# The RWKV recurrence of a decoder trunk as 64 by 64 tiles of the array, both heads of a pair together

## The chip, the cores and the metric

The kernel runs on one core of one Trainium2 chip. The metric is the device time of one execution in microseconds: 2238.92 us, the median of 3 runs (2235.21 to 2239.05). The profile shows one further execution of its own.

A core has TensorE (PE, with its weight loads listed apart as PEld), VectorE (DVE), ScalarE (ACT), GpSimd (POOL), and SyncE, whose queue (SP) issues the DMAs here. PE multiplies from SBUF into PSUM, which holds eight banks of 128 partitions by 512 float32 values.

## The reference, cut to what matters

The kernel computes a trunk of two layers on 512 positions of 1024 features. Each layer adds half a SwiGLU feed-forward, a mixer, and half a feed-forward again. The mixer of layer 0 is RWKV-7 with 12 heads of 64, beside an attention of 4 heads to a memory of 256 positions; that of layer 1 is a dilated attention and the same kind of memory attention. The part that the change rewrites is the recurrence of layer 0:

```python
def step(state, inp):
    r_t, w_t, k_t, v_t, kk_t, a_t = inp
    sa = jnp.einsum('bhvk,bhk->bhv', state, -kk_t)
    state = (state * w_t[:, :, None, :]
             + sa[..., None] * (kk_t * a_t)[:, :, None, :]
             + v_t[..., None] * k_t[:, :, None, :])
    return state, jnp.einsum('bhvk,bhk->bhv', state, r_t)
```

Its state is 64 by 64 for each head. The outputs are then normalised by head, get a bonus term, and are gated.

## The kernel before

Everything is feature-major: a tile is 128 features (two heads of 64) by 512 positions. The feed-forward layers (`ffn`) and the projections (`dense`, line 399) split each float32 operand into two halves of 12 bits and take three products of whole 128 by 128 blocks with 512 columns; one step of `dense` issues three such matmuls and yields. They read as `fps` (feed-forward) and `mm` (mixer) in the profile. The small products of the recurrence are plain float32 matmuls, and each of them leaves two records of PE.

The mixer of layer 0 (`mixer_a`, line 584) handles the 12 heads as 6 pairs, one pair to a tile of 128 features. It is written as strands, Python generators that emit instructions in steps: `projections` (key, receptance and value of pair j), `prepare` (decay, normalised keys, everything by position, `rwkv_prepare`, line 728), two strands `scan(0)` and `scan(1)` that run `rwkv_solve` (line 801) on the first and the second head of each pair, `finish` (`rwkv_finish`, line 865), two strands of memory attention, and a first pass of the output projection. `weave` (line 294) emits each time the first strand whose next step can start by the clock of `Meter` (line 216), which adds up an estimated cost of each instruction (`cost`, line 225). All strands share the PSUM banks `mm` (2), `sc` (4) and `py` (2). The pairs are coupled: `prepare` of pair j waits until the output of pair j-2 is there (line 683), the projections of pair j wait until pair j-2 is prepared, and `finish` takes the pairs one by one.

The recurrence is cut into 8 chunks of 64 positions; a block is two chunks, 128 positions. For one head, `rwkv_solve` does this:

- Products within the chunks (`AR` with `beta` and `kappa`): 64 by 64 tiles, whose results are masked by DVE onto the diagonal squares of 128 by 128 matrices (`products`, the profile's `prod`) that are zero elsewhere and were cleared once at the start.
- The inverse of a triangular matrix by doubling (`LEVELS`, 2 to 32): at each of five levels DVE turns 32 by 32 squares of `TT`, PE multiplies by `MA` for each of the four blocks (128 by 128, the profile's `sc<-tx,prod`), DVE masks, PE multiplies again (`sc<-TT,tx`), and DVE adds.
- `SA` (the turned `AR` of this head, and what the chunk reads of its own values), and `wu`, the solution for both.

`rwkv_finish` turns `beta` and `kappa` to positions on partitions, in a copy for each chunk of a block with zeros in the other chunk's rows (`betatok`, `kappatok`), and for each head in turn: the readout matrices (`pt`), the transitions `G`, and what each chunk adds to the state, gathered in the `py` bank. A loop over the chunks then carries the state of both heads: PE multiplies `G` by `H`, ACT scales into the next `H` (one copy a head), PE reads out. Group norm, bonus and gate follow.

Of the kernel before, what the change touches and what calls it, by code (L numbers as in the profile page):

```python
# [17 lines left out]
P = 128  # L18
# [5 lines left out]
HD = 64  # L24
# [12 lines left out]
# ---------------------------------------------------------------- constants of shapes alone  # L37
# [12 lines left out]
def constants():  # L50
    f = np.float32
    i = np.arange(P)
    same = (i[:, None] // HD == i[None, :] // HD).astype(f)
    s, t = i[:, None], i[None, :]
    chunk = s // C == t // C
    strict, incl = (chunk & (s < t)).astype(f), (chunk & (s <= t)).astype(f)
    lvl = []
    for b in LEVELS:
        lvl.append(((s // (2 * b) == t // (2 * b)) & (s // b % 2 == 1) & (t // b % 2 == 0)).astype(f))
    first = ((s // 2 == t // 2) & (s % 2 == 0) & (t % 2 == 1)).astype(f)  # L60
    ident = np.eye(P, dtype=f)
    stack = np.concatenate([np.eye(HD, dtype=f)] * 2, 0)
    cols = [ident, same, 1.0 - same, np.ones((P, P), f), strict, incl, first, *lvl, stack]
# [17 lines left out]
CONST_W = [P, P, P, P, 2 * P, P, *([P] * len(LEVELS)), HD]  # L81
# [10 lines left out]
def swapped(n):  # L92
    """Feature order with the two heads of each 128-row tile exchanged."""
# [50 lines left out]
# ---------------------------------------------------------------- kernel  # L144
# [17 lines left out]
def wide(t):  # L162
    return t.unsqueeze(1).broadcast_to([P, 4, P])
# [6 lines left out]
class Operand:  # L170
    """Both halves of x * gain for each 128 features, and the sum of squares of x, as the tiles of x come."""
# [31 lines left out]
    def rstd(self, ps):  # L203
        """1 / sqrt(mean over features + eps) on every partition."""
# [11 lines left out]
class Meter:  # L216
    """Estimates when each engine gets through what has been emitted, to choose the order of emission."""

    def __init__(self):
# [3 lines left out]
        self.banks = set()  # L223

    def cost(self, engine, op, out, ins, extra):
        """extra: operands that are one value per partition, and sums over the free size."""
# [4 lines left out]
        if engine == "tensor":  # L231
# [3 lines left out]
            return max(n * passes * 0.000417 * (0.6 if out.shape[0] < P else 1), 0.055) + 0.003  # L235
# [24 lines left out]
    def follow(self, slots, n, tile):  # L260
        """The tile takes the place of the one n tiles before it in slots."""
# [22 lines left out]
class Core:  # L284
    """The engines, with a meter on each."""
# [44 lines left out]
class Net:  # L330
# [30 lines left out]
    def warm(self):  # L361
        """The table of the first activations, ahead of their data."""
# [17 lines left out]
    # -- weights: one chunk is [128, nb, 128]; both halves of each value  # L380
# [34 lines left out]
    def split_into(self, hi, lo, src, gain=None):  # L415
        """hi + lo = src * gain exactly, each of 12 bits."""
# [8 lines left out]
    def add_state(self, old, j, ps, nexts, dst, scale=None, permute=False, x=None):  # L425
        """Tile j of x, to the operands that follow and to DRAM. scale: half of what the columns of ps lack."""
# [14 lines left out]
    # -- x + 1/2 SwiGLU(x)  # L441
# [46 lines left out]
    # -- keys and values of the memory  # L488
# [13 lines left out]
    def memory_kv(self, layer, tmp, bank, operand, out):  # L502
        """out: keys [128, 2, 256] by feature and values [128, 2, 256] by position."""
# [19 lines left out]
    def head_norm(self, out, t, gain, tmp, bank, n):  # L523
        """RMS norm over the 64 rows of each head."""
# [58 lines left out]
    # -- layer 0: RWKV-7 and memory attention  # L583
    def mixer_a(self, xin, u, kv, mid, nexts, dst, after):
        nc, tc = self.nc, self.tc
        w = self.ap["wa_in"]
        with ExitStack() as ctx:
# [10 lines left out]
            self.tok = {}  # L598
            for n in ("beta", "kappa"):
                self.tok[n] = pool.tile([P, 4, 2, P], F32, name=f"{n}tok")  # L600
                nc.gpsimd.memset(self.tok[n], 0.0)

            # zero outside the chunks' squares
            self.products = [[pool.tile([P, 4, 2, P], F32, name=self.nm("prod")) for _ in range(2)] for _ in range(2)]
            for two in self.products:
                for t in two:
                    nc.gpsimd.memset(t, 0.0)

# [14 lines left out]
            self.lora = {}  # L623
            self.krv = [None] * NPAIR
# [4 lines left out]
            def shifted(ps, m, out):  # L629
                """Projection m over the rms, mixed with the position before."""  # L630
# [7 lines left out]
            def projections():  # L638
# [89 lines left out]
    def rwkv_prepare(self, j):  # L728
        """Decay, keys and the rest by position, for heads 2j and 2j + 1."""
# [6 lines left out]
        # E[., c, t] is the decay over chunk c before position t, Ei the inverse of that after it  # L736
        zw = self.bank("sc")
        pe.matmul(zw, lora[:HD, 0], self.lo[:HD], start=True, stop=True)
# [3 lines left out]
        yield WAIT  # L742
        za = self.bank("sc")
        pe.matmul(za, lora[HD:, 0], self.lo[HD:], start=True, stop=True)
# [56 lines left out]
    def rwkv_solve(self, j, e):  # L801
        """What the chunks of head 2j + e read of the state at their start and of their own values."""
# [4 lines left out]
        mine, vals = own(e), own(1 - e)  # L807
        # products within the chunks, on the diagonal of MA[:, block] = A_b', A_k' and MB[:, block] = B_b', B_k'
        MA, MB = self.products[e]
        for b0 in (0, 2):  # L810
            ps = self.bank("sc", (P, 2, 2, 2, C))
            for b in range(2):
                for q, t in enumerate((beta, kappa)):
                    for c in range(2):
                        at = (b0 + b) * P + c * C
                        pe.matmul(ps[own(c), b, q], t[mine, at:at + C], AR[mine, b0 + b, :, own(c)], start=True,
                                  stop=True, skip_group_check=True)
            yield FREE
            for i, m in enumerate((MA, MB)):
                for c in range(2):  # L820
                    mask = self.mprod[own(c), i * P + c * C:i * P + (c + 1) * C]
                    vec.tensor_tensor(m[own(c), b0:b0 + 2, :, own(c)], ps[own(c), :, :, i],
                                      mask.unsqueeze(1).unsqueeze(1).broadcast_to([C, 2, 2, C]), op=ALU.mult)
            yield FREE
        yield WAIT
        ps = self.bank("sc", (P, 4, P))
        for b in range(4):
            pe.transpose(ps[:, b, :HD], AR[mine, b, 0], self.ident[mine, mine])
        SA = self.big("SA", 2, (P, 4, P))
        act.activation(SA[:, :, mine], ps[:, :, :HD], AF.Copy)  # L830
        # inverse of I - A_b by doubling the blocks of its diagonal
        TT = self.big("TT", 2, (P, 4, P))
        gp.tensor_tensor(TT, MA[:, :, 0], wide(self.first), op=ALU.mult)
        gp.tensor_tensor(TT, TT, wide(self.ident), op=ALU.add)
        yield WAIT
        for lv in LEVELS:
            # blocks of at most 32 lie on the diagonal: turning each 32 by 32 square turns the whole
            tn = self.big("tx", 3, (P, 4, P))
            vec.transpose(tn.rearrange("p b u -> p (b u)"), TT.rearrange("p b u -> p (b u)"))
            yield WAIT  # L840
            ps = self.bank("sc", (P, 4, P))
            for b in range(4):
                pe.matmul(ps[:, b], MA[:, b, 0], tn[:, b], start=True, stop=True, skip_group_check=True)
            X = self.big("tx", 3, (P, 4, P))
            vec.tensor_tensor(X, ps, wide(getattr(self, f"lvl{lv}")), op=ALU.mult)
            yield WAIT
            ps = self.bank("sc", (P, 4, P))
            for b in range(4):
                pe.matmul(ps[:, b], X[:, b], TT[:, b], start=True, stop=True, skip_group_check=True)
            vec.tensor_tensor(TT, TT, ps, op=ALU.add)  # L850
            yield WAIT
        ps = self.bank("sc", (P, 4, P))
        for b in range(4):
# [367 lines left out]
```

## Time and profile before

| | us |
|---|---|
| runs: median (lowest, highest) | 2238.92 (2235.21, 2239.05) |
| the profiled execution: its span | 2236.6 |
| layer-0 mixer, first projection to the start of its last outputs | 385 to 880 |
| `bv` written, the last step of `prepare`, first and last pair | 441.5, 775.5 |
| layer-1 mixer, about | 1640 to 1880 |

The span lies 2.3 us under the median of the runs. The page counts PE, its weight loads and the three other engines as busy by the union of their instructions. A record's length is a latency; records overlap, also on one tile of the array, so what one costs is the distance to the start of the next. In the groups, the numbers after the count are the group's busy time and the mean length of one record in ns. The form `64*64` names the rows and columns of the array that a matmul uses; `sc<-TT,tx` names what it writes and reads. A helper records every operation, so all instructions carry its line (L276). The rows that carry the argument stand in the prediction.

### The profile page before, as it was taken

To read this page: it belongs to the slowest core of one execution; us is meant where nothing else is said; L and a number is where in the kernel's file an instruction comes from. 1 tells how busy PE (TensorE), PEld (TensorE's weight loads), DVE (VectorE), ACT (ScalarE), POOL (GpSimd) and SP (SyncE) were. 2 spreads that over 40 slices of the span, in tenths; PEclk is the share of its full clock that TensorE was granted. 3 is DMA by queue.
4 is the path that set the end of the run, shared out by engine and by line. 5 is a ranking of instruction groups with operands and counts; after the bars stand their busy time and mean duration, and the time that the engine had idled before them with its cause. 6 is when DMAs were issued, how large, how long until landed. Compare 5 with 4: busy or idle time off the path is not lost.

```text
span 2236.6 us, 29471 instructions
## 1 busy us (share of the span) xinstructions
PE 2206.0 (99%) x11174; PEld 1779.8 (80%) x11174; DVE 1066.1 (48%) x1556; ACT 843.8 (38%) x1492; POOL 603.3 (27%) x520
## 2 busy tenths in 40 slices
PE   8999999999999999999999999999999999999999
PEld 6888888688777877778888888888877677888887
DVE  5333334576877874633343443333355675333332
ACT  6333333323323444433343343333334544333321
POOL 2222223632333113322222222222232224222221
PEclk9999999989999999999999999999999999999999
DMA  5333344200100005436334443333451125333342
GB/s 195 98 96 95 104 136 139 76 24 22 32 28 13 12 22 180 153 95 182 95 109 132 136 136 98 96 96 113 134 143 52 41 90 191 100 98 96 94 137 80
DMA packets 130621, 221.97 MB, mean 99 GB/s; under 512 B 14232, under 2 KB 31824, under 8 KB 130480
## 3 DMA queue, kind: packets, MB, share of 16 engines
q1 hardware_dynamic: 130480, 220.09, 32.6%
q8 instruction: 88, 1.44, 0.3%
q14 instruction: 53, 0.43, 0.1%
HBM read 203.15 MB, written 21.61 MB: 100 GB/s over the span
## 4 chain that ended last, share of the span: by engine, by line
PE 94%; DVE 3%; ACT 1%; POOL 1%; issue 1%; DMA 1%; SPq 0%; POOLq 0%; ACTq 0%; DVEq 0%
PE fps L276 65%; PE sc L276 14%; PE mm L276 12%; PE py L276 4%; DVE tmp L276 1%; DVE tx L276 0%; DVE prod L276 0%; DVE krv L276 0%; POOL wlo L276 0%; ACT uh L276 0%; POOL sq L276 0%; DMA raw<-w 0%; DMA x<-xT 0%; DVE x L276 0%; DMA tmp<-xd 0%
## 5 line engine op out<-in xcount | busy, mean ns | idle before, releaser
L276 POOL TENSOR_TENSOR wlo<-raw,whi 128x512 fp32r<-128x512 f32 (+3 forms) x404 | 496.6, 1231 | 1460.3 <-ACT whi L276 1427.8
L276 ACT ACTIVATE whi<-raw 128x512 fp32r<-128x512 f32 (+3 forms) x684 | 416.3, 610 | 943.9 <-PE fps L276 787.3
L276 PE MATMUL fps<-uh,whi 128*128 128x512 f32 x1408 | 551.5, 392 | 8.3 <-ACT whi L276 8.3
L276 PE MATMUL fps<-uh,wlo 128*128 128x512 f32 x1408 | 550.6, 391 | 2.3 <-POOL wlo L276 2.1
L276 PE MATMUL fps<-ul,whi 128*128 128x512 f32 x1408 | 548.9, 390 | 0.0
L276 DVE TENSOR_TENSOR wlo<-raw,whi 128x512 fp32r<-128x512 f32 x280 | 199.8, 714 | 344.5 <-ACT whi L276 333.3
L276 PEld LDWEIGHTS fps<-uh,whi 128*128 128x128 f32 x1408 | 264.9, 188 | 68.5 <-ACT whi L276 11.7
L276 PEld LDWEIGHTS fps<-uh,wlo 128*128 128x128 f32 x1408 | 264.9, 188 | 61.6 <-POOL wlo L276 5.3
L276 PEld LDWEIGHTS fps<-ul,whi 128*128 128x128 f32 x1408 | 264.8, 188 | 55.4 <-issue 0.7
L276 PE MATMUL fps<-hh,whi 128*128 128x512 f32 x704 | 273.9, 389 | 0.0
L276 PE MATMUL fps<-hl,whi 128*128 128x512 f32 x704 | 273.9, 389 | 0.0
L276 PE MATMUL fps<-hh,wlo 128*128 128x512 f32 x704 | 273.9, 389 | 0.0
L276 DVE TENSOR_TENSOR gs<-fps,rstd 128x512 f32<-128x512 f32 x88 | 60.5, 690 | 324.5 <-PE fps L276 324.5
L276 PEld LDWEIGHTS fps<-hh,wlo 128*128 128x128 f32 x704 | 132.1, 188 | 27.7
L276 PEld LDWEIGHTS fps<-hh,whi 128*128 128x128 f32 x704 | 132.1, 188 | 27.5
L276 PEld LDWEIGHTS fps<-hl,whi 128*128 128x128 f32 x704 | 132.1, 188 | 27.1
L276 PE MATMUL mm<-uh,whi 128*128 128x512 f32 x280 | 121.3, 434 | 1.5 <-ACT uh L276 1.1
L276 PE MATMUL mm<-ul,whi 128*128 128x512 f32 x280 | 117.9, 421 | 0.0
L276 DVE TENSOR_TENSOR hm<-fps,gs 128x512 f32<-128x512 f32 x88 | 60.6, 691 | 120.1 <-PE fps L276 115.8
L276 PE MATMUL mm<-uh,wlo 128*128 128x512 f32 x280 | 115.0, 411 | 0.0
L276 DVE RECIPROCAL tmp<-tmp 128x128 f32<-128x128 f32 x112 | 99.4, 920 | 16.6 <-ACT tmp L276 16.5
L276 DVE TENSOR_TENSOR hl<-hm,hh 128x512 fp32r<-128x512 f32 x88 | 77.5, 883 | 50.7 <-ACT hh L276 50.6
(256 smaller groups left out, 2612.2 us busy)
## 6 DMA issues: line engine op xcount, KB each, us to landing
raw<-w SPq DMA_DIRECT2D x512, 256.0 KB, 2.7
raw<-wa_in SPq DMA_DIRECT2D x44, 256.0 KB, 2.8
xd<-x SPq DMA_DIRECT2D x40, 256.0 KB, 2.5
tmp<-xd SPq DMA_DIRECT2D x32, 256.0 KB, 3.4
xin<-xd SPq DMA_DIRECT2D x32, 256.0 KB, 4.3
raw<-w_kv SPq DMA_DIRECT2D x24, 256.0 KB, 3.0
raw<-w SPq DMA_DIRECT2D x32, 128.0 KB, 2.4
raw<-wmem SPq DMA_DIRECT2D x16, 256.0 KB, 2.7
```

Source lines behind the costliest of these rows:

```text
L276: r = f(*args, **kw)
```

## The change

The recurrence goes to 64 by 64 tiles of the array throughout, and both heads of a pair are done together, side by side in the columns of a tile.

- `rwkv_solve(j)` takes a pair. Positions of a chunk of either half of a block lie on partitions 0 to 63 or 64 to 127, the heads beside each other along the columns. The products of `beta`, then of `kappa`, fill one bank for each head and are masked by one DVE operation a head into `mb` and `mk`; the cleared 128 by 128 matrices are gone. `TT`, its transposes and its masks are `[128, 8, 64]` for both heads. Each level is 16 products of 64 by 64 in place of 4 of 128 by 128 a head, on the two diagonal tiles of the array, into one bank.
- The transposes of `beta` and `kappa` move from `rwkv_finish` into `rwkv_solve`, without the zero rows. `SA` is one tile for both heads with a flag `shared` around its use; `AR` is turned whole.
- `rwkv_finish` computes `pt` and `G` for both heads in two banks `kg`, one for each half of the blocks, and gathers readouts and state terms in two banks `py`, again one for each half. In the state loop ACT makes one copy `H` of 128 partitions a step for both heads.
- The strands `scan(0)` and `scan(1)` take the even and the odd pairs in place of the first and the second heads.
- In `rwkv_prepare` the products `zw` and `za` are issued next to each other.
- `Meter.cost` has no factor 0.6 for narrow outputs, a least cost of 0.105 in place of 0.055, a division by the number of tiles that a block of code declares with `packed`, and 0.1 for each change between packed and other matmuls. It also plans the mixer of layer 1.
- The masks in the block of constants are 64 columns wide in place of 128 (1088 columns in all, from 1600). Comments are removed.

```diff
@@ Meter.cost
-            return max(n * passes * 0.000417 * (0.6 if out.shape[0] < P else 1), 0.055) + 0.003
+            small = self.ways > 1
+            turn, self.small = 0.1 * (small != self.small), small
+            return turn + max(n * passes * 0.000417, 0.105) / self.ways + 0.003
@@ mixer_a
-            def scan(e):
-                for j in range(NPAIR):
+            def scan(par):
+                for j in range(par, NPAIR, 2):
                     yield from until(lambda: self.made[j])
-                    yield from self.rwkv_solve(j, e)
+                    yield from self.rwkv_solve(j)
@@ rwkv_prepare
+        zw, za = self.bank("sc"), self.bank("sc")
+        with self.packed(2):
+            pe.matmul(zw, lora[:HD, 0], self.lo[:HD], start=True, stop=True)
+            pe.matmul(za, lora[HD:, 0], self.lo[HD:], start=True, stop=True)
@@ rwkv_solve
+        spots = [(e, b, c) for e in range(2) for b in range(4) for c in range(2)]
...
+        for t, name in ((beta, "mb"), (kappa, "mk")):
+            ps = [self.bank("sc", (P, 4, 2, C)) for _ in range(2)]
+            with self.packed(4):
+                for b in range(4):
                     for c in range(2):
+                        for e in range(2):
+                            at = b * P + c * C
+                            pe.matmul(ps[e][own(c), b], t[own(e), at:at + C], AR[own(e), b, :, own(c)], start=True,
+                                      stop=True, skip_group_check=True)
+            m = self.big(name, 2, (P, 2, 4, 2, C))
+            for e in range(2):
+                vec.tensor_tensor(m[:, e], ps[e], mask, op=ALU.mult)
...
-            for b in range(4):
-                pe.matmul(ps[:, b], MA[:, b, 0], tn[:, b], start=True, stop=True, skip_group_check=True)
+            ps = self.bank("sc", (P, 8, C))
+            with self.packed(2):
+                for e, b, c in spots:
+                    i = 4 * e + b
+                    pe.matmul(ps[own(c), i], M[0][own(c), e, b, 0], tn[own(c), i], start=True, stop=True,
+                              skip_group_check=True)
...
@@ rwkv_finish
+        py = [self.bank("py", (P, 2, 4, C)) for _ in range(2)]
+        with self.packed(4):
+            for b, c, e in spots:
+                pe.matmul(py[c][own(1 - e), 0, b], wu[own(c), e, b, C:], Mb[own(c), e, b, 1], start=b == 0, stop=False,
+                          skip_group_check=True)
...
+        for i in range(1, NCH):
+            b, c = divmod(i - 1, 2)
+            act.activation(H[:, i], py[c][:, 1, b], AF.Copy, scale=E[:, i - 1, C:])
             yield WAIT
...
+                        pe.matmul(py[c][own(e), 1, b], G[own(e), c, b], H[own(e), i], start=False, stop=i >= NCH - 3,
+                                  skip_group_check=True)
```

More of the change, by code (lines that the diff above doesn't have):

```diff
@@ L53, in constants @@
     same = (i[:, None] // HD == i[None, :] // HD).astype(f)
[L54 to L57, printed above, removed]
+    ident = np.eye(P, dtype=f)
+    cols = [ident, same, 1.0 - same, np.ones((P, P), f)]
+    s, t = np.arange(C)[:, None], np.arange(C)[None, :]
+    pairs = [s < t, s <= t, (s // 2 == t // 2) & (s % 2 == 0) & (t % 2 == 1)]
     for b in LEVELS:
[L59 to L63, printed above, removed]
+        pairs.append((s // (2 * b) == t // (2 * b)) & (s // b % 2 == 1) & (t // b % 2 == 0))
+    pairs.append(s == t)
+    cols += [np.concatenate([m.astype(f)] * 2, 0) for m in pairs]
     hot, neg = np.zeros((32, 9, 256), f), np.full((12, 9, 256), NEG, f)
@@ L597, in mixer_a @@
             nc.gpsimd.memset(self.reset.rearrange("p (c u) -> p c u", u=C)[:, :, 0:1], 0.0)
[L598 to L607, printed above, removed]
             def derived(name, m, b=None):
@@ L824, in rwkv_solve @@
             yield FREE
         yield WAIT
[L826 to L834 removed]
+        Ab = M[0][:, :, :, 0].rearrange("p e b u -> p (e b) u")
@@ L835, in rwkv_solve @@
+        TT = self.big("TT", 2, (P, 8, C))
+        gp.tensor_tensor(TT, Ab, wide(self.first), op=ALU.mult)
+        gp.tensor_tensor(TT, TT, wide(self.stack), op=ALU.add)
+        turned = {}
+        for n in ("beta", "kappa"):
+            ps = self.turned(lambda b: d[n][:, b * P:(b + 1) * P])
+            turned[n] = self.big(f"{n}tok", 2, (P, 4, P))
+            act.activation(turned[n], ps, AF.Copy)
+            yield FREE
         yield WAIT
         for lv in LEVELS:
-            tn = self.big("tx", 3, (P, 4, P))
+            tn = self.big("tx", 3, (P, 8, C))
@@ L845, in rwkv_solve @@
+            X = self.big("tx", 3, (P, 8, C))
             vec.tensor_tensor(X, ps, wide(getattr(self, f"lvl{lv}")), op=ALU.mult)
             yield WAIT
-            ps = self.bank("sc", (P, 4, P))
-            for b in range(4):
-                pe.matmul(ps[:, b], X[:, b], TT[:, b], start=True, stop=True, skip_group_check=True)
+            ps = self.bank("sc", (P, 8, C))
+            with self.packed(2):
+                for e, b, c in spots:
+                    i = 4 * e + b
+                    pe.matmul(ps[own(c), i], X[own(c), i], TT[own(c), i], start=True, stop=True, skip_group_check=True)
@@ L850, in rwkv_solve @@
             vec.tensor_tensor(TT, TT, ps, op=ALU.add)
             yield WAIT
-        ps = self.bank("sc", (P, 4, P))
-        for b in range(4):
-            pe.matmul(ps[:, b, :HD], MA[:, b, 1], vt[:, b, vals], start=True, stop=True, skip_group_check=True)
-        act.activation(SA[:, :, vals], ps[:, :, :HD], AF.Copy)
-        yield WAIT
-        ps = self.bank("sc", (P, 4, P))
-        for b in range(4):
-            pe.matmul(ps[:, b], TT[:, b], SA[:, b], start=True, stop=True, skip_group_check=True)
@@ new lines, in rwkv_solve @@
+        with self.packed(2):
+            for e, b, c in spots:
+                pe.matmul(ps[own(c), 4 * e + b], M[1][own(c), e, b, 0], vt[own(c), b, own(1 - e)], start=True, stop=True,
+                          skip_group_check=True)
+        act.activation(SA[:, :, :, C:], ps.rearrange("p (e b) u -> p e b u", e=2), AF.Copy)
+        yield WAIT
+        self.shared = False
+        wu = self.big("WU", 2, (P, 2, 4, P))
+        ps = [self.bank("sc", (P, 4, P)) for _ in range(2)]
+        with self.packed(2):
+            for e, b, c in spots:
+                pe.matmul(ps[e][own(c), b], TT[own(c), 4 * e + b], SA[own(c), e, b], start=True, stop=True,
+                          skip_group_check=True)
@@ L865, in rwkv_finish, with packed @@
+        for e in range(2):
+            act.activation(wu[:, e], ps[e], AF.Copy)
+        yield WAIT
+        self.solved[j] = wu, M, turned
+    @contextmanager
+    def packed(self, ways):
+        self.meter.ways = ways
+        yield
+        self.meter.ways = 1
     def rwkv_finish(self, j, y):
@@ L870, in rwkv_finish @@
         E, AR, vt, bv = d["E"], d["AR"], d["vt"], d["bv"]
-        for n in ("beta", "kappa"):
-            ps = self.turned(lambda b: d[n][:, b * P:(b + 1) * P])
-            for c in range(2):
-                act.activation(self.tok[n][c * C:(c + 1) * C, :, c], ps[c * C:(c + 1) * C], AF.Copy)
-            yield WAIT
-        tb, tk = self.tok["beta"], self.tok["kappa"]
-        yield from until(lambda: (j, 0) in self.solved)
-        py, G = [None] * 2, [None] * 2
-        pt = self.big("pt")
@@ new lines, in rwkv_finish @@
+        wu, (Mb, Mk), tok = self.solved[j]
+        tb, tk = tok["beta"], tok["kappa"]
+        spots = [(b, c, e) for b in range(4) for c in range(2) for e in range(2)]
+        kg = [self.bank("sc", (P, 2, 4, C)) for _ in range(2)]
+        with self.packed(4):
+            for b, c, e in spots:
+                pe.matmul(kg[c][own(e), 0, b], wu[own(c), e, b, :C], Mb[own(c), e, b, 1], start=b == 0, stop=False,
+                          skip_group_check=True)
+            for b, c, e in spots:
+                if 0 < 2 * b + c < NCH - 1:
+                    pe.matmul(kg[c][own(e), 1, b], wu[own(c), e, b, :C], tb[own(c), b, own(e)], start=False,
+                              stop=b == 3, skip_group_check=True)
@@ new lines, in rwkv_finish, with readout @@
+        H = self.big("H", 1, (P, NCH, C))
+        def readout(i):
+            b, c = divmod(i, 2)
+            for e in range(2):
+                pe.matmul(py[c][own(1 - e), 0, b], H[own(e), i], pt[own(e), c, b], start=False, stop=i >= NCH - 2,
+                          skip_group_check=True)
+        for i in range(1, NCH):
+            b, c = divmod(i - 1, 2)
+            act.activation(H[:, i], py[c][:, 1, b], AF.Copy, scale=E[:, i - 1, C:])
+            yield WAIT
+            b, c = divmod(i, 2)
+            with self.packed(4):
+                if i > 1:
+                    readout(i - 1)
+                if i < NCH - 1:
+                    for e in range(2):
+                        pe.matmul(py[c][own(e), 1, b], G[own(e), c, b], H[own(e), i], start=False, stop=i >= NCH - 3,
+                                  skip_group_check=True)
+                if i == NCH - 1:
+                    readout(i)
@@ L930, in rwkv_finish @@
             yield WAIT
         y0 = self.tmp()
-        for e in range(2):
-            act.activation(y0[own(1 - e)], py[e][own(1 - e)], AF.Copy)
+        for c in range(2):
+            act.activation(y0.rearrange("p (b c u) -> p b c u", c=2, u=C)[:, :, c], py[c][:, 0], AF.Copy)
         yield WAIT
```

114 lines of the change are left out of this document (36 added, 78 removed).

## The prediction

> **What bounds the kernel now.** I read the profile page first: its span, the engines' busy shares, and the shares of the chain that ended last.
>
> ```profile
> span 2236.6 us, 29471 instructions
> PE 2206.0 (99%) x11174; PEld 1779.8 (80%) x11174; DVE 1066.1 (48%) x1556; ACT 843.8 (38%) x1492; POOL 603.3 (27%) x520
> ...
> PE fps L276 65%; PE sc L276 14%; PE mm L276 12%; PE py L276 4%; DVE tmp L276 1%; DVE tx L276 0%; DVE prod L276 0%; DVE krv L276 0%; POOL wlo L276 0%; ACT uh L276 0%; POOL sq L276 0%; DMA raw<-w 0%; DMA x<-xT 0%; DVE x L276 0%; DMA tmp<-xd 0%
> ```
>
> TensorE (PE) is busy nearly always and carries the chain. 65% of the chain is the feed-forward layers (`fps`), which the change leaves alone. What it rewrites lies in the layer-0 mixer. So the next view is the busy time by stretch: the mixer from its first projection to its last output but one, then the five intervals between the six pairs, then the tail. The columns are PE, weight loads, DVE, ACT, POOL, the granted clock, DMA.
>
> ```profile
> 385.00:880.00 495.00, 482.80 (x3436) 379.73 (x3435) 345.06 (x554) 175.11 (x353) 155.82 (x157) 0.97 0.13 40
> 442.00:776.00 334.00, 331.82 (x2568) 266.96 (x2568) 249.67 (x395) 109.56 (x212) 97.23 (x92) 0.97 0.08 23
> 776.00:880.00 104.00, 99.03 (x657) 73.94 (x656) 62.05 (x119) 42.84 (x107) 18.62 (x19) 0.95 0.21 67
> ```
>
> The mixer takes 495 us. PE is busy for 483 of them, DVE for 345 (70%). The view of waits, PE alone, 385 to 880 us, lists seven waits that sum to 11.3 us; the first and the last are
>
> ```profile
> PE sc L276 <- DVE tmp L276: 4.9, 1, 4.9
> ...
> PE mm L276 <- DVE p L276: 0.2, 1, 0.2
> ```
>
> Every PE microsecond taken out of the mixer is therefore worth up to a microsecond. A pair is ready for its scan when `bv` is written:
>
> ```profile
> L276 DVE TENSOR_TENSOR bv<-sc,krv x6: 690/692/692, 441.5 to 775.5; 128x512 f32<-128x512 f32 x6
> ```
>
> Six pairs from 441.5 to 775.5: one each 66.8 us. Two pairs are in flight at most, since `prepare` of pair j waits for the output of pair j-2.
>
> **The change part by part.** The costs are PE records; each float32 matmul leaves two. From the groups by line and shape, 385 to 880 us (records, busy us, mean ns):
>
> ```profile
> L276 PE MATMUL sc<-TT,tx 128*128 128x128 f32 x480 | 65.7, 281 | 2.1 <-DVE tx L276 1.9
> L276 PE MATMUL sc<-tx,prod 128*128 128x128 f32 x480 | 63.7, 277 | 0.7 <-DVE tx L276 0.5
> L276 PE MATMUL sc<-AR,beta 64*64 64x128 f32 x192 | 24.3, 302 | 0.0
> L276 PE MATMUL sc<-AR,kappa 64*64 64x128 f32 x192 | 24.2, 296 | 0.0
> L276 PE MATMUL py<-WU,betatok 128*64 128x64 f32 x168 | 20.7, 225 | 0.0
> L276 PE MATMUL py<-vt,kappatok 128*64 128x64 f32 x168 | 20.2, 222 | 0.0
> L276 PE MATMUL sc<-lo,lora 64*128 64x512 f32 x24 | 15.3, 722 | 0.0
> L276 PE MATMUL py<-prod,WU 128*128 128x128 f32 x96 | 13.4, 280 | 0.0
> L276 PE MATMUL sc<-SA,TT 128*128 128x128 f32 x96 | 13.3, 280 | 0.0
> L276 PE MATMUL sc<-betatok,WU 128*64 128x128 f32 x96 | 13.1, 279 | 0.0
> L276 PE MATMUL py<-prod,vt 128*64 128x128 f32 x96 | 13.0, 279 | 0.0
> L276 PE MATMUL sc<-vt,prod 128*128 128x64 f32 x96 | 12.0, 268 | 0.0
> L276 PE MATMUL sc<-cst,AR 64*128 64x64 f32 x48 | 6.0, 250 | 0.0
> ```
>
> The mean is a latency and records overlap, so the price of one is its distance to the next. From the timeline of PE (start, length, form, count):
>
> ```profile
> 461.22 1.05 PE L276 MATMUL sc<-tx,prod 128*128 128x128 f32 x8
> ...
> 577.95 0.27 PE L276 MATMUL py<-pt,H 64*64 64x64 f32 x1
> 577.96 0.27 PE L276 MATMUL py<-H,G 64*64 64x64 f32 x1
> 577.97 0.27 PE L276 MATMUL py<-pt,H 64*64 64x64 f32 x1
> 577.97 0.32 PE L276 MATMUL sc<-AR,beta 64*64 64x128 f32 x1
> ...
> 704.08 0.28 PE L276 MATMUL py<-vt,kappatok 128*64 128x64 f32 x2
> 704.19 0.28 PE L276 MATMUL py<-WU,betatok 128*64 128x64 f32 x2
> ...
> 846.98 0.50 PE L276 MATMUL mm<-uh,whi 128*128 128x512 f32 x1
> 847.41 0.27 PE L276 MATMUL py<-pt,H 64*64 64x64 f32 x1
> ...
> 847.67 0.51 PE L276 MATMUL mm<-ul,whi 128*128 128x512 f32 x1
> 848.11 0.27 PE L276 MATMUL py<-pt,H 64*64 64x64 f32 x1
> ```
>
> Eight records of 128 columns in 1.05 us, the last one 0.28 long: (1.05 - 0.28)/7 = 0.111 us each. Two of 64 columns in 0.115: 0.058. At 577.95 four records start within 0.02 us, on four different 64 by 64 tiles: four tiles do run at once. So I price two tiles at half of these (0.055 and 0.029), four at a quarter (0.028 and 0.0145). A visit to 64 by 64 tiles between dense records is not free: from 847.41 to 848.11 passes 0.70 us, in which one dense record (about 0.23, as at full pace in the feed-forward) and two turns of the tiles (0.12) are work. The rest, 0.35 us, is the price of going over and back.
>
> - Levels of the inverse. Removed: 960 records x 0.111 = 107. Added: 5 levels x 2 x 16 matmuls x 2 records x 6 pairs = 1920, on the two diagonal tiles, x 0.029 = 56; and 60 visits x 0.35 = 21, where none was before. Net -30.
> - Products (`AR`): 384 records stay; from two tiles to four, 21 to 10.5; some 24 visits become 12. Net -15.
> - Reading the values and solving (`vt,prod` and `SA,TT`): 192 x 0.111 = 21 becomes 192 x 0.029 + 192 x 0.055 + 6 visits = 18. Net -3.
> - In `finish`: 288 records of 128 columns x 0.111 + 336 x 0.058 = 51 becomes 336 + 744 records on four tiles, 1080 x 0.0145 = 16, and 2 for visits. Net -34. If the queue feeds no more than a record in 0.025 us, it is -22; I keep -34, for the four starts at 577.95 lie far closer than either.
> - Transposes of `AR`: 48 half ones (6.0 busy) become 24 whole ones of 0.111. Net -3.
> - `zw` and `za` side by side in the two row halves: half of 15.3. Net -7.
> - State loop: the same seven steps of up to eight records. ACT makes one copy a step instead of two; nothing on PE.
> - The cleared tiles go: six memsets of POOL at the mixer's start, of the size of the four in the first row below, 5.7 us beside dense work of PE; 0, and at most -6 if POOL is late there. A shorter constant block lands earlier: -1 at most.
> - `Meter.cost` changes the order in layer 1 too (no 0.6 for narrow outputs). PE's waits there (1640 to 1880 us) are five and sum to 3.6; the longest is the second row below. So 0, within 4 either way.
>
> ```profile
> L276 POOL MEMSET prod<- 128x1024 f32 x4 | 3.6, 956 | 0.0
> ...
> PE mm L276 <- DVE x L276: 1.5, 1, 1.5
> ```
>
> Sum: -92 of PE time, if PE stays as full as it is. That is the lower bound: 2236.6 - 92 = 2145; the runs' median lies 2.3 over the profiled span, so 2147.
>
> DVE gains as well. Two of its groups:
>
> ```profile
> L276 DVE STREAM_TRANSPOSE tx<-TT 128x512 f32<-128x512 f32 x60 | 41.7, 700 | 0.7 <-POOL TT L276 0.4
> ...
> L276 DVE TENSOR_TENSOR prod<-sc,cst 64x256 f32<-64x256 f32 x96 | 40.5, 422 | 12.9 <-PE sc L276 11.3
> ```
>
> The first is one of three operations per level that now serve both heads at once: 60 become 30, thrice, and at 0.7 us that is -62. The second, the masks of the products, falls from 96 to 24 of full size, 40.5 to some 17. From 345 us DVE goes to about 260; it will not be the next bound.
>
> **What is late next.** Two things take a part back. First the loop of a pair (prepare, solve, finish, then prepare of the pair after next). PE's part per pair falls from 66.8 to 66.8 - 92/6 = 51.5. But the chain of one pair's levels is as long as that of one head was, and with the heads merged fewer strands stand ready to fill PE. The interval lies between 51.5 and 66.8; I take 55, nearer to PE's need, since PE lost only 2 us in these 334. Five intervals then lose 18 of the saving, and the tail, which has hardly any projections left, 3.
>
> Second the clock. The rows by stretch of the last state loop, and of the products at the start:
>
> ```profile
> 443.70:447.10 3.40, 3.40 (x27) 2.93 (x28) 0.95 (x2) 1.87 (x3) 0.71 (x2) 0.50 0.27 77
> 846.50:849.90 3.40, 3.39 (x27) 1.94 (x27) 0.00 (x0) 1.71 (x6) 0.00 (x0) 1.00 0.31 117
> 849.90:860.10 10.20, 10.20 (x32) 5.83 (x32) 0.00 (x0) 2.74 (x6) 1.27 (x1) 0.50 0.12 31
> ```
>
> From 846.5 PE is busy 3.39 of 3.40 us, and yet the granted clock is 0.50 from 849.9 on for 10.2 us. Those 3.4 us are the pattern shown above: one dense record, then a few small ones. Weighted by the part of the array in use, a 0.70 us cycle holds 0.23 + 4 x 0.058/4 = 0.29, so about 0.4. A level group after the change has 0.93 us on two quarter tiles and 0.35 of changeover: 0.46/1.28 = 0.36, unless dense records stand beside it. So stretches of this kind become common. I charge three more drops of some 11 us at half clock, half of it lost: +16. The Trainium skill ("TensorE: Matmul & The Clock Gate", HAM oscillation) lets the clock fall for PE-idle gaps over about 3.4 us; by that rule alone no such drop would come, and the sum would stand 16 us lower. The row at 846.5 speaks against it: 3.39 of 3.40 busy, and a drop.
>
> -92 + 18 + 3 + 16 - 1 = -56 on 2236.6: 2181 in the profile, **2183** as a median of the runs. Its own range is 2150 to 2215.
>
> **The rivals.**
> - All of the saving stays (PE full, no new drop): 2147, up to 2150. For it: 2 us of waits in 334 now. Against: fewer strands, less area.
> - One bank, two row halves. The level groups write both diagonal tiles into one PSUM bank; in the rows of before the tiles that run at once write different banks. If they take turns, levels cost 1920 x 0.058 = 111, solving 11 and 10 more: 72 back. PE then fills as now, so only the clock's 16 stays: -92 + 72 + 16 = -4, 2235 (2215 to 2245). The Trainium skill ("TensorEngine Tiling (Array Packing)", Gotcha 1: PSUM Pressure) states that different row tiles cannot access the same bank simultaneously; no row of before shows two row tiles in one bank, so the trace does not decide.
> - The chain of a pair bounds. If an interval stays near 64, 62 of the 77 us over five intervals are lost: -92 + 62 + 3 + 16 = -11, 2228. For it: prepare of j waits for the end of j-2. Against: PE, not a wait, fills the interval now.
> - Slower by the clock. Once at half, it came back only after a stretch of dense records: at 443.7 us PE is busy 3.40 of 3.40 with products on small tiles, and the clock stays at 0.50. If the mixer's small tiles hold it there, each us at half loses half a us. From 92 - 21 = 71 lost, or 142 us at half clock, the change stops paying; with 250 us of the 418 between 442 and 860 the loss is 125, PE is the bound throughout (only the tail's 3 stay): -92 + 3 + 125 = +36, 2275.
> - The change does not do what it says: tiles queue one after another. Levels 111 + 21 - 107 = +25, products 43 - 25 = +18, solving +13, finish 63 + 2 - 51 = +14, transposes -3: +67, 2306. The four starts at 577.95 speak against it.
>
> **How the numbers follow.** Forecast 0.50; all of it 0.10; one bank 0.12; chain 0.10; clock 0.14; no overlap 0.04. Of 0.2% either way (4.5 us, about what a measurement of this kernel can tell): faster holds forecast and all of it (0.60), 0.09 of the chain and 0.08 of the bank: 0.77. Same holds 0.03 of the bank, 0.01 of the chain, 0.02 of a mild clock loss: 0.06. Slower holds the rest of the clock (0.12), no overlap (0.04) and 0.01 of the bank: 0.17. The range 2145 to 2255 leaves out a little below and the heavier clock losses and no overlap above: about 0.2.
>
> **What would show it.** Level groups of 32 records in about 1.1 us (two tiles at once), or 2 us (one bank, or no overlap). Groups of `finish` with starts 0.015 to 0.03 apart. Six `bv` in intervals of about 55 us; if these are 64 while PE shows waits for DVE or ACT, the chain bounds. The mean granted clock of the mixer, 0.97 over 495 us now (some 30 us at half): near 0.93 as forecast (some 63 us), under 0.82 for a loss. DVE busy in the mixer near 260 instead of 345. The forecast is wrong if PE's waits in the mixer exceed 50 us, or if the clock stays at half through whole pairs.

## The result, and the profile after

The changed kernel takes 2172.16 us (median of 4 runs, 2169.05 to 2176.88), the kernel before in the same series 2237.07 (2232.28 to 2239.05). The ratio is 0.9713, with a 95% interval of 0.9696 to 0.9731: faster by 65 us. The forecast was 2183, its own range 2150 to 2215.

From the profile page of the changed kernel, the span and the engines:

```profile
span 2167.3 us, 32275 instructions
## 1 busy us (share of the span) xinstructions
PE 2100.8 (97%) x12734; PEld 1675.1 (77%) x12734; DVE 983.3 (45%) x1394; ACT 821.6 (38%) x1430; POOL 581.1 (27%) x502
```

The profiled span falls by 69.3 us, and PE's busy time by 105: PE is a little less full than it was. Where the time went is seen by stage (distances between first matmuls of the stages):

| stage | before, us | after, us | difference |
|---|---|---|---|
| up to the first projection of layer 0's mixer | 385.7 | 386.8 | +1.1 |
| mixer of layer 0, to its last outputs | 493.7 | 407.2 | -86.5 |
| from there to the keys of layer 1 | 777.8 | 777.4 | -0.4 |
| mixer of layer 1, keys to next feed-forward | 212.2 | 224.0 | +11.8 |
| last feed-forward | 367.2 | 371.9 | +4.7 |

So the part that was rewritten gives 86.5 us, and 16.5 of them are lost in layer 1, whose code the change does not touch. The busy time by stretch, mixer of layer 0: before (one row), then after with the stretches between the first and the last `bv`, the tail, and two short ones for later (PE, weight loads, DVE, ACT, POOL, granted clock, DMA).

```profile
385.70:879.40 493.70, 481.50 (x3429) 378.65 (x3427) 344.38 (x552) 173.90 (x351) 154.67 (x155) 0.97 0.13 39
```

```profile
386.80:794.00 407.20, 368.10 (x4990) 269.65 (x4988) 262.32 (x390) 150.26 (x288) 136.99 (x137) 0.98 0.15 48
442.00:709.80 267.80, 240.75 (x3841) 177.20 (x3843) 182.95 (x259) 90.74 (x159) 91.74 (x84) 0.98 0.09 29
709.80:794.00 84.20, 77.85 (x945) 54.36 (x946) 47.25 (x91) 39.51 (x97) 12.12 (x14) 0.98 0.25 80
588.00:591.40 3.40, 1.26 (x34) 1.03 (x32) 3.40 (x5) 0.53 (x1) 2.15 (x3) 1.00 0.09 33
591.40:594.80 3.40, 3.40 (x43) 2.83 (x39) 3.40 (x6) 0.80 (x2) 1.71 (x2) 0.50 0.25 82
```

PE's busy time in this mixer falls by 113 us, DVE's by 82. The six `bv` now run from 441.6 to 709.8, an interval of 53.6 us in place of 66.8:

```profile
L278 DVE TENSOR_TENSOR bv<-sc,krv x6: 628/692/693, 441.6 to 709.8; 128x512 f32<-128x512 f32 x6
```

The view of PE's waits there, which had seven rows (13 waits) with 11.3 us in all, has fifteen rows (40 waits) with 38.8 now. The longest four rows of the changed kernel (us in total, times, longest):

```profile
PE sc L278 <- DVE tx L278: 13.0, 12, 2.1
PE sc L278 <- ACT tmp L278: 6.0, 5, 2.5
PE sc L278 <- DVE tmp L278: 5.5, 1, 5.5
PE py L278 <- issue: 3.3, 4, 1.2
```

The level groups wait for DVE now (`tx`): PE is ahead of the chain more often, but not by much. From the timeline of PE, a level group with dense records after it, the next level group, and two groups of `finish`:

```profile
561.63 1.15 PE L278 MATMUL sc<-tx,mb 64*64 64x64 f32 x32 [0.85 <-ACT whi L278]
562.71 0.50 PE L278 MATMUL mm<-uh,wlo 128*128 128x512 f32 x1
563.04 0.40 PE L278 MATMUL mm<-uh,whi 128*128 128x512 f32 x1
...
563.74 0.40 PE L278 MATMUL mm<-uh,whi 128*128 128x512 f32 x1
564.07 1.15 PE L278 MATMUL sc<-TT,tx 64*64 64x64 f32 x32
...
536.02 0.65 PE L278 MATMUL py<-mb,WU 64*64 64x64 f32 x32
536.49 0.65 PE L278 MATMUL py<-mk,vt 64*64 64x64 f32 x32
```

A level group takes 1.08 us from its start to the next dense record (562.71 - 561.63), way out included. The dense records on either side of it take 0.33 in place of 0.23 (563.04 - 562.71, and 564.07 - 563.74). In `finish`, 32 records on four tiles take 0.47 us: 0.0147 each, against a price of 0.0145 in the prediction.

### The profile page after: what moved, and what is told of

Its sections match the earlier page's. It is cut to its first block, busy times and chain, and to the rows that moved or that the text cites. A ratio compares the mean times of both kernels' runs of the same rounds, so it can differ in the third digit from the quotient of the medians.

```text
span 2167.3 us, 32275 instructions
## 1 busy us (share of the span) xinstructions
PE 2100.8 (97%) x12734; PEld 1675.1 (77%) x12734; DVE 983.3 (45%) x1394; ACT 821.6 (38%) x1430; POOL 581.1 (27%) x502
## 4 chain that ended last, share of the span: by engine, by line
PE 63%; DVE 2%; ACT 1%; issue 1%; POOL 0%; DVEq 0%; ACTq 0%; POOLq 0%
PE fps L278 51%; PE mm L278 6%; PE sc L278 5%; PE py L278 2%; DVE tmp L278 0%; DVE x L278 0%; DVE ul L278 0%; DVE prob L278 0%; DVE qn L278 0%; ACT tmp L278 0%; DVE mpr L278 0%; DVE dmx L278 0%; DVE tx L278 0%; ACT krv L278 0%; ACT L278 0%
```

## The experiments

Two questions were open: why layer 1 lost 16.5 us, and what in layer 0 the gain hangs on. Each ratio is to the kernel before, run in the same series (medians 2235.9 to 2238.6 us). The changed kernel was not run again beside them, so a difference to its 2172 us is known to some 3 us.

The granted clock moves the time of a program too: of 19 runs of the kernel before in one series, one at a mean clock of 0.997 took 2230.8 us and one at 0.991 took 2239.2. Where two versions differ in clock, runs of equal clock are compared below.

**The cost in the planner: the kernel before with the new cost.**

```diff
-            return max(n * passes * 0.000417 * (0.6 if out.shape[0] < P else 1), 0.055) + 0.003
+            return max(n * passes * 0.000417, 0.105) + 0.003
```

> The kernel before, with the new cost of a matmul (no factor 0.6, least cost 0.105; nothing is declared packed there). Theory one, the planner: layer 1 loses 12 to 17 us here too, layer 0 moves by less than 8 either way: 2243 to 2260. Rival, what is carried over from the new mixer: layer 1 stays at 579 us, and the time within 5 us of 2237.

Measured: 2257.49 us, ratio 1.0085 (1.0057 to 1.0113), 19 us slower. PE and DVE have the same number of instructions as before (11174 and 1556); their order differs. The mixer of layer 1, from its keys to the next feed-forward, in the kernel before and in this run:

```profile
1657.20:1869.40 212.20, 210.06 (x1034) 155.31 (x1032) 137.05 (x241) 109.81 (x228) 57.16 (x49) 1.00 0.26 81
```

```profile
1662.10:1890.20 228.10, 220.00 (x1033) 159.77 (x1032) 140.05 (x241) 110.78 (x229) 53.68 (x48) 0.97 0.23 74
```

212.2 us become 228.1: PE stands idle for 8 us in place of 2, and the clock is 0.97 in the mean. From the keys to the end the loss is 19.8 us (579.4 to 599.2), a little more than theory one had; the mixer of layer 0 moves by 3.8 (493.7 to 497.5). The planner's theory holds without any of the new tiles.

In the changed kernel the longest wait of layer 1 is the one that this run has too, to the tenth of a microsecond; PE waits once more at the start of the last feed-forward:

```profile
PE sc L278 <- DVE mpr L278: 4.3, 3, 3.6
PE fps L278 <- DVE wlo L278: 3.9, 1, 3.9
```

**The old cost in layer 1 alone, in the changed kernel.**

```diff
+            if self.narrow:
+                return max(n * passes * 0.000417 * (0.6 if out.shape[0] < P else 1), 0.055) + 0.003
...
+            self.meter.narrow = True
             weave(self.meter, [memory(0), memory(1), dilated(0), dilated(1), dilated(2), settle(), projections(), first_pass()])
```

> The changed kernel, with the old cost of a matmul (factor 0.6 for narrow outputs) for the planner in the mixer of layer 1 alone. Theory one, the planner: the 16.6 us that the profile loses from the first matmul of layer 1's keys to the end (579.4 before, 596.0 after) come from the new cost, which orders that mixer otherwise. Then these 596 us go back to 580, and the median from 2172 to about 2156. Rival, what is carried over: the new layer-0 mixer leaves other clocks and buffers behind it, and the cost is innocent. Then 2172, within 3.

Measured: 2157.0 us, ratio 0.9639 (0.9616 to 0.9662), 15 us under the changed kernel. Layer 1 is back at its old length to the tenth:

```profile
1575.70:1787.90 212.20, 210.06 (x1034) 155.32 (x1032) 137.04 (x241) 109.72 (x228) 57.06 (x49) 1.00 0.24 81
```

What the new layer-0 mixer leaves behind is innocent. In layer 1 no matmul is declared packed and none is as cheap as 0.105, so the whole effect is the factor 0.6 for narrow outputs. Without it the planner charges 0.21 us for a product of probabilities and values in place of 0.13. The trace has two records of 0.109 each for it (`py<-probT,vt`), so the new number is the truer one, and it gives the worse order.

**The old cost everywhere, in the changed kernel.** The return line as it was in the kernel before, in layer 0 too.

> The changed kernel, with the old cost of a matmul everywhere: no division by the number of tiles, no price for a change of form, factor 0.6 for narrow outputs. Theory one, the gain in layer 0 is in the work on PE and not in the plan: that mixer stays within 10 us of its 409 us (386 to 795), layer 1 gets its 16 us back, 2156 to 2166. Rival: the new plan is part of the gain, the level groups that the old cost takes for twice as long as they are crowd out the rest, and the mixer of layer 0 loses 20 us or more: over 2176.

Measured: 2147.81 us, ratio 0.9607 (0.9583 to 0.9631), and once more with more rounds:

> The changed kernel with the old cost everywhere once more, in more rounds and beside the one above: 2148 within 4 if the first measurement holds, a ratio of 0.958 to 0.963; 2157 if it was no better than the old cost in layer 1 alone.

2151.01 us, ratio 0.9614 (0.9598 to 0.9629). This is the best version found, some 21 us under the changed kernel. That the retuned cost of layer 0 is worth nothing is clear; that it costs something is likely (2148 and 2151 against 2157), but the intervals touch. The two profiles of this one program differ in layer 0 by 5 us. The first stands at half clock for 13.6 us of it (6.8, 3.4 and 3.4), the second for 27.2; half of the difference, 6.8 us, is enough to account for it:

```profile
386.30:787.90 401.60, 366.17 (x4990) 266.60 (x4988) 263.78 (x390) 153.30 (x290) 134.19 (x137) 0.98 0.15 48
```

```profile
386.00:792.90 406.90, 370.93 (x4988) 270.92 (x4987) 263.70 (x390) 153.45 (x289) 134.22 (x137) 0.97 0.15 48
```

**Which part of the cost.** The old cost, divided by the number of tiles where matmuls are declared packed, and no price for a change of form:

```diff
+            return max(n * passes * 0.000417 * (0.6 if out.shape[0] < P else 1) / self.ways, 0.055 / self.ways) + 0.003
```

> The changed kernel, with the old cost of a matmul (factor 0.6, least cost 0.055), divided by the number of tiles where matmuls are declared packed; no price for a change of form. The old cost everywhere gave 2148, the old cost in layer 1 alone 2157; this asks which part of the new cost takes the 9 us of layer 0. Theory one, the price for a change of form (it makes the planner put dense work elsewhere): without it 2146 to 2152, layer 0 about 402 us. Rival, the division: layer 0 stays at 407 to 413 us, 2154 to 2160. Third: layer 0 differs between executions by as much as this, and nothing can be told: between.

Measured: 2166.53 us, ratio 0.9682 (0.9662 to 0.9702), worse than either theory had it. The mixer of layer 0 takes 424.6 us, and its mean clock is 0.94:

```profile
386.10:810.70 424.60, 382.03 (x4989) 276.88 (x4988) 262.00 (x390) 148.27 (x286) 135.47 (x137) 0.94 0.15 47
```

This mixer stands at half clock for 51.2 us, against 13.6 and 27.2 in the two profiles of the old cost; half of the difference, 12 to 19 us, is the most that the clock costs of the 18 to 23 that the mixer loses. At an equal clock of 0.992 one run of this version took 2161.7 us, two of the old cost 2151.0 and 2153.4, so some 9 us stay without the clock. The division alone is thus a loss, and the version that neither divides nor charges for a change of form is the best of the three. Its cost for a level group is 16 x (0.064 + 0.003) = 1.1 us, close to the 1.08 measured; with the division it is 16 x (0.032 + 0.003) = 0.56. Whether the price for a change of form makes good for the division in the changed kernel was not tested alone: the two also differ in the factor 0.6 and in the least cost.

**Tiles in the levels alone, each head by itself, in the kernel before.**

```diff
-            for b in range(4):
-                pe.matmul(ps[:, b], MA[:, b, 0], tn[:, b], start=True, stop=True, skip_group_check=True)
+            for b in range(4):
+                for c in range(2):
+                    pe.matmul(ps[own(c), b], MA[own(c), b, 0, own(c)], tn[own(c), b], start=True, stop=True,
+                              skip_group_check=True)
```

`TT`, `tn` and `X` are `[128, 4, 64]` here, the second product and the solution likewise.

> The kernel before, with the level groups and the solution on 64 by 64 diagonal tiles, but each head by itself (120 groups of 16 records in place of 120 of 8 whole-array ones; the three DVE operations of a level work on 256 columns a head). Theory one: half of what the levels gain on PE is that both heads share a group and so a visit to the small tiles. With two visits in place of one, levels cost 1920 x 0.025 to 0.029 and 120 x 0.35, 90 to 98 us against 107, and the time falls by 5 to 18 us: 2219 to 2232. Rival: tiles alone do it, visits are nearly free: 50 us less on PE, 2190 to 2205. Third: visits dearer than priced eat it all, over 2237.

Measured: 2211.75 us, ratio 0.9887 (0.9855 to 0.992), 27 us faster: between theory one and the rival. From the timeline of PE, groups of one head, and two heads that fell into one visit:

```profile
599.80 0.68 PE L277 MATMUL sc<-TT,tx 64*64 64x64 f32 x16
600.32 0.63 PE L277 MATMUL sc<-tx,prod 64*64 64x64 f32 x16
602.55 0.68 PE L277 MATMUL sc<-TT,tx 64*64 64x64 f32 x16 [0.25 <-DVE tx L277]
605.06 0.68 PE L277 MATMUL sc<-tx,prod 64*64 64x64 f32 x16
```

At 599.80 the two strands stand in one visit, the second head's records 0.52 us after the first's. Not each of the 120 groups pays for a way of its own, which theory one had assumed: by the trace they lie in 97 visits, a visit being an unbroken stretch of 64 by 64 records. Tiles in the levels alone give about two fifths of the 65 us. The rest was not taken apart by runs; the heads together, the groups of `finish` and the products are what is left of the change.

**One tile after the other in the levels, in the changed kernel.** The same 16 products a group, all on one diagonal tile, then all on the other.

```diff
+        by_tile = [(e, b, c) for c in range(2) for e in range(2) for b in range(4)]
...
-                for e, b, c in spots:
+                for e, b, c in by_tile:
```

> The changed kernel, with the 16 products of each level group in another order: eight on one diagonal tile, then eight on the other, in place of one on each in turn. Theory one: tiles overlap only where neighbours in the program lie on different tiles. The first 16 records then take 0.058 us each and the next 16 too, 1.86 us a group instead of 0.93: 60 x 0.93 = 56 us more on PE, and the time goes up by 40 to 56 us, 2212 to 2228. Rival: the array looks far enough ahead to start the second tile's records beside the first's: within 10 us of 2172.

Measured: 2228.26 us, ratio 0.9964 (0.9946 to 0.9981): 56 us given back by the order of a loop. The timeline has a group of 32 records at 1.90 us in place of 1.15, and the mean clock of the mixer falls to 0.92:

```profile
606.26 1.90 PE L278 MATMUL sc<-tx,mb 64*64 64x64 f32 x32
```

```profile
386.30:854.50 468.20, 437.09 (x4989) 331.72 (x4988) 263.68 (x390) 150.53 (x287) 135.90 (x137) 0.92 0.13 42
```

60 x 0.75 = 45 us is the missing overlap, and the mixer takes 61 more. A clock of 0.92 means 468 x 2 x 0.08 = 75 us at half speed, against some 16 in the changed kernel (407 x 2 x 0.02); half of the difference, 30 us, is the most that it costs, and PE's idle time is 8 us less (39.1 to 31.1). At an equal clock of 0.988 one run of each took 2218.2 and 2176.9 us: some 41 of the 56 us stay without the clock.

Each of the seven drops of the clock in this mixer comes after a stretch of 3.4 us in which PE stood idle for 0.9 us or more. What is new is how long the clock stays down while PE is busy. The stretch before the last drop, and the one at half clock behind it:

```profile
774.60:778.00 3.40, 2.00 (x8) 1.00 (x7) 2.02 (x5) 1.12 (x5) 0.00 (x0) 1.00 0.00 0
778.00:808.70 30.70, 30.31 (x167) 21.40 (x168) 10.74 (x26) 6.59 (x20) 0.45 (x1) 0.50 0.02 7
```

From 774 to 809 us 138 records are those of the levels, on one tile at a time, and 4 are dense.

**The products and finish in turn.** Tile by tile in place of one on each of four tiles.

```diff
-        spots = [(b, c, e) for b in range(4) for c in range(2) for e in range(2)]
+        spots = [(b, c, e) for c in range(2) for e in range(2) for b in range(4)]
```

The loops over `b`, `c` and `e` of the products are turned alike.

> The changed kernel, with the products of the chunks and the groups of finish ordered tile by tile (all matmuls of one tile, then the next) in place of one on each of four tiles in turn. Theory one, as for the levels: finish goes from 1080 x 0.016 = 17 to 1080 x 0.058 = 63 us, the products from 17 to 384 x 0.109 = 42: 71 us more on PE at most, some of it won back where the queue looks ahead: 40 to 71 us, 2212 to 2243. Rival: the array looks ahead over 16 records, within 10 us of 2172.

Measured: 2189.78 us, ratio 0.9795 (0.9774 to 0.9816), 18 us slower than the changed kernel: less than theory one, more than the rival. The runs on a tile are shorter here, eight records in place of sixteen, and records overlap at the seams:

```profile
541.97 1.14 PE L278 MATMUL py<-mb,WU 64*64 64x64 f32 x26
...
543.01 0.22 PE L278 MATMUL py<-mk,vt 64*64 64x64 f32 x1
543.01 0.22 PE L278 MATMUL py<-mb,WU 64*64 64x64 f32 x1
```

(1.14 - 0.22)/25 = 0.037 us a record, between 0.058 (no overlap) and 0.0147 (four tiles). The two lines at 543.01 are such a seam: the next product starts on its tile while the last records of this one still start on theirs. PE's idle time in this mixer is 12 us less than in the changed kernel (27.0 against 39.1), which hides a part of the cost.

**Twice the visits.** One whole-array matmul in the middle of each level group; it computes nothing that is used.

```diff
                 for e, b, c in spots:
                     i = 4 * e + b
+                    if (e, b, c) == (1, 0, 0):
+                        pe.matmul(ps[:, 7], self.ident, tn[:, 7], start=True, stop=True, skip_group_check=True)
```

The second product of a level has the same with `TT` in place of `tn`.

> The changed kernel, with one whole-array matmul (128 by 128 on 64 columns, two records, into columns that the group overwrites afterwards) in the middle of each of the 60 level groups: twice the visits to the small tiles. It computes nothing that is used. Theory one: a visit costs 0.35 us and the matmul 0.12 to 0.22, 60 x (0.47 to 0.57) = 28 to 34 us more on PE, and the time goes up by 20 to 34 us: 2192 to 2206. Rival: a visit is nearly free, only the two records count: 7 to 13 us, 2179 to 2185.

Measured: 2201.39 us, ratio 0.9842 (0.9824 to 0.9859), 29 us slower: theory one. From the timeline of PE:

```profile
568.99 0.68 PE L278 MATMUL sc<-tx,mb 64*64 64x64 f32 x16 [0.85 <-DVE tx L278]
569.61 0.43 PE L278 MATMUL sc<-tx,cst 128*128 128x64 f32 x2
569.97 0.68 PE L278 MATMUL sc<-tx,mb 64*64 64x64 f32 x16
570.58 0.50 PE L278 MATMUL mm<-ul,whi 128*128 128x512 f32 x1
```

Half a group, the matmul and half a group take 0.62 + 0.36 + 0.61 us from start to start, in place of 1.08: 0.51 more for each of 60, of which the matmul's own columns are 0.11, at the 0.111 us that 128 columns take. A visit costs 0.40 us by this, a little over the 0.35 of the prediction.

**The low-rank products side by side, in the kernel before.** Only `zw` and `za` are issued next to each other.

> The kernel before, with only the step of prepare changed: the two half-height products of the low-rank factors issued next to each other. Theory one: both row halves run at once, 24 records of 0.53 us become 12 steps, 6 to 7 us less on PE, and the time falls by 4 to 7 us: 2230 to 2233. Rival: the plan moves and hides or outweighs it: within 3 us of 2237, or above.

Measured: 2230.29 us, ratio 0.9971 (0.9961 to 0.9981), 6 us faster, the number that theory one gave. The packing does what it was priced at: the group's busy time is 7.7 us in place of 15.3.

```profile
L276 PE MATMUL sc<-lo,lora 64*128 64x512 f32 x24 | 7.7, 724 | 0.0
```

That the time fell by as much is partly luck, for two other things moved. The mixer of this run:

```profile
386.90:875.10 488.20, 468.18 (x3430) 372.80 (x3429) 347.59 (x552) 175.54 (x354) 152.31 (x155) 0.99 0.13 39
```

PE stands idle for 20.0 us in place of 12.2, and the clock is 0.99 in place of 0.97. Its ten runs had a mean clock of 0.996 to 0.998, the 19 of the kernel before in this series 0.991 to 0.997. At an equal clock of 0.997 this version took 2229.6 to 2231.3 us and the kernel before 2230.8 to 2231.7: about 1 us. So the rival holds as well: the new plan takes back most of what the packing saves, and why its clock is better was not found out.

## Why the prediction was right, point by point

The time came out 11 us under the forecast, inside its own range. The mechanism was right: less work on PE, by tiles that run at once, with a part of it lost to waits. That the number came so close is partly luck, since layer 0 gave 31.5 us more than forecast and layer 1 lost 16.5 that were forecast at nothing. In the mixer of layer 0 the sum was -92 of work, +21 of waits and +16 of clock, -55 in all; the profiles show -105, +27 and -8.5, which is -86.5.

- **PE is the bound, and its prices.** Right. The prices from the rows of before hold: four tiles at 0.0147 us (priced 0.0145), the two low-rank products at half. Two diagonal tiles do run at once into one bank: a group of 32 records takes 1.08 us, and 1.83 with one tile after the other. That rival falls. With 0.10 in the dense record on either side, the levels cost 60 x (1.08 + 0.10 + 0.10) = 77 us, as priced. DVE went to 262 us in the mixer, forecast 260.
- **The sum of 92.** Too small by 13. PE's busy time fell by 113.4 us, about 8.5 of them by the clock (half of the 17 us less at half clock), so its work fell by about 105. One part of the 13 is the state loop, forecast at nothing on PE: the busy time of its two groups (`py<-pt,H` and `py<-H,G`) falls from 41.9 to 25.0 us, and by the distances between starts it costs about 10 us in place of 19. The rest was not assigned. (`finish` has 1056 records on four tiles, not 1080.)
- **The loop of a pair, and the waits.** The interval was forecast at 55 us and is 53.6. It holds five times, 7 us more than forecast. The tail is 20 us shorter (103.9 to 84.2), where 12 was the forecast. PE's idle time in the mixer grew by 27 us (12.2 to 39.1), where 18 and 3 were charged; 25 of the 27 lie between the first and the last `bv`. So the chain of a pair takes back what it was charged and a little more, but it does not bound.
- **The clock.** The term that was mis-sized most: the charge of 16 us did not come. The prediction took the drop at 849.9, behind a stretch with PE busy, as the pattern of the new kernel, and charged three more drops of some 11 us. The mixer of before stood at half clock for 34.1 us, in two drops of 23.9 and 10.2; after, there are four, of 6.8, 3.4, 3.4 and 3.4 us. The first drop of before, then the 3.4 us ahead of each drop of after (that ahead of 591.4 is shown above):

```profile
436.90:460.80 23.90, 21.39 (x98) 14.18 (x99) 14.41 (x24) 5.12 (x9) 8.72 (x8) 0.50 0.07 21
```

```profile
434.40:437.80 3.40, 0.00 (x0) 0.00 (x0) 3.33 (x5) 0.00 (x0) 1.70 (x3) 1.00 0.00 0
451.40:454.80 3.40, 1.56 (x33) 1.34 (x34) 1.09 (x2) 0.25 (x1) 0.94 (x1) 1.00 0.02 5
731.30:734.70 3.40, 1.61 (x9) 0.85 (x7) 2.32 (x8) 1.17 (x5) 0.00 (x0) 1.00 0.01 2
```

After the change PE waited for half of each such stretch or more (ahead of the drop at 591.4 it was busy for 1.26 of 3.40 us), and no drop came out of a busy stretch. At 591.4 PE is busy throughout again, more than half of the time with two diagonal tiles, and the clock is back after 3.4 us. PE busy on small tiles, as the prediction had it, thus brought none of these drops; whether the chip counts busy time or the part of the array in use was not measured. The risk was real all the same: with one tile at a time the clock stayed at half for 75 us, about half of the 142 at which the slower rival (given 0.14) put the end of the gain. The 8.5 us gained are luck of these two executions: over the whole kernel the mean clock was 0.988 to 0.992 after and 0.991 to 0.997 before, and the same layer-0 program had 0.96 in its mixer in the run with the old cost in layer 1:

```profile
386.00:798.90 412.90, 375.09 (x4989) 273.32 (x4988) 262.31 (x390) 150.62 (x287) 136.82 (x137) 0.96 0.15 47
```

- **Layer 1.** Wrong: 0, within 4 either way, was forecast; it was 16.5 lost. The prediction looked at PE's waits there, found them near nothing, and took that for safety. But a stage with hardly any waits has little to win from another order, and much to lose. The cost function was part of the change and reached a second mixer, where a truer price of an instruction gave a worse order.

So 31.5 us more than forecast came from layer 0, 24.5 of them the clock, and 16.5 were lost in layer 1, with 4 of difference left in the start and in the way of counting. A forecast that had priced layer 1 at its loss and left the rest as it was would have said 2200.

## What to carry to other kernels

Matmuls of 64 by 64 on different tiles of the array run side by side when the program puts neighbours on different tiles: the order of one loop is worth 56 us here, where the whole change gives 65; some 41 of the 56 stay at equal clock. A visit to small tiles between whole-array matmuls costs about 0.35 to 0.4 us here, so groups should be as long as the dependences allow; putting both heads of a pair into one group is what does that here.

A planner's cost of an instruction is a knob of the order, not a measurement. Retune it stage by stage, and look at each stage that it plans.

## What the runs showed of the hardware that was not expected

- Two diagonal 64 by 64 tiles write to one PSUM bank at once: 1.08 us for 32 records, against 1.83 in turn. The Trainium skill ("TensorEngine Tiling (Array Packing)", Gotcha 1: PSUM Pressure) states that different row tiles cannot access the same bank simultaneously; here, with outputs on different partitions, they do, and the measurement decides.
- Once down, the clock can stay at half with PE busy: 30.31 of 30.70 us with level products on one 64 by 64 tile at a time, while with two tiles at once it was back after 3.4 us, at 594.8 in the changed kernel. Whether the small area, the small records or something else keeps it down was not tested. The granted clock differs between executions of one program too, 0.98 and 0.97 for the same mixer.
- PE stood idle four times, 3.3 us in all, with nothing that the profile shows to wait for (`issue`), in the long groups of `finish` with 120 records on four tiles. What it waits for there stays open.
